# Low parts of the mixer's mx, mo and mv weights on GpSimd, and a later due count for a finished selection

## The chip, the cores and the metric

The kernel runs on one core of one Trainium2 chip. The metric is the device time of one execution in microseconds (us); a row of the trace gives times from the start of the profiled execution's span.

## The reference

A block of two layers (a causal convolution branch, a dilated attention branch, each with a gated per-layer embedding), then a feed-forward part (SwiGLU), a mixer, and a second feed-forward part, for 512 tokens of width 1024 in float32. The change lies in the mixer. It projects the normalised input to all that its two halves need, and the sparse attention half selects keys per query:

```python
def block(args):                       # 128 queries, block bi
    logits = jnp.einsum('bqhd,bsd->bqhs', iq_blk, ik)
    score = jnp.einsum('bqhs,bqh->bqs', jax.nn.relu(logits), iw_blk) * idx_scale
    score = jnp.where(allowed[None], score, -jnp.inf)
    # the k_sel = 128 largest scores of each query are the keys that it may attend to;
    # softmax attention of 8 heads (2 key/value heads) over those keys
...
# mLSTM half: mx -> causal convolution of 4 taps -> SiLU -> q, k;  mo -> sigmoid output gate;
# mv -> values;  input and forget gates from 8 more columns
# out = two gates * (attention @ wo, mLSTM @ wo) + residual
```

## The kernel before, in words

Every float32 weight comes from memory in pieces of 128x1024 elements (512 KB, "raw", four buffers) and is split into a high part `whi` and a low part `wlo` (six buffers each). ScalarE writes `whi` (L117, a rounding copy), and another engine writes `wlo = raw - whi` (L119). A product of 512 columns is then three matmuls, high by high, low by high and high by low (L281, L282, L283). In what follows ACT is ScalarE, DVE is VectorE, POOL is GpSimd and PE is TensorE.

`Stream.split` chooses the engine of `wlo`: GpSimd where the piece's index is in `POOL_LO`, its key in `POOL_KEYS` or its full name in `POOL_MORE` (most pieces of the feed-forward parts), and DVE otherwise. The mixer's pieces come as aq (queries), mx (mLSTM input), mo (output gate), mv (values), then the two gates gb and ga and the output weights.

The main products of a unit run in a loop that ticks; at each tick side work is given out at fixed rates. `k.t` counts main products. The side work of the attention half: `score(tb)` makes the index scores of query block tb (products L1079/L1080, rectified copies on ACT L1871, weighted sums on DVE L1878 and L1880); `select(tb)` takes the 128 largest by 16 rounds of a maximum of 8 (L1888) and a replacement (L1889) on DVE, and L1891 turns the result into an additive mask; `attend()` goes through 4 blocks of 8 heads in stages: s1 (products L1079/L1080 into a bank of PSUM), s1b (DVE adds the mask and takes the maximum, L1914, which also frees the bank; L1918 negates it; ACT takes the exponential, L1919), s2 (transposes L1932, ACT copies them, L1935), s3 (products with the values, L1948). `attend()` doesn't give out s1 of a block before its selection is in `SEL`. READY is 8, and two other kinds of results (the queries "AQ" among them) already become due that many main products after they were given out.

The mLSTM half: `mx_evac` scales each mx product into an SBUF tile (DVE, L1994), starts a convolution on ACT (L1998), adds three taps on DVE (L2002, two operands from SBUF) and takes the SiLU (L2004, its own ACT table, loaded by an `ACT_TABLE_LOAD`). The queries' norm goes through a sum on DVE (L1094, L1096), a power on GpSimd (L276) and a scaling (L1098, L1100); then PE transposes (L1850) and ACT and DVE split the result (L1069, L1070).

There are eight banks of PSUM. The order of the instructions on every engine is set by a scheduler with a timeline model when the kernel is built, so a change of an engine or of a due count moves instructions on all engines. Line numbers from L1893 on are larger by one after the change (L1914 becomes L1915).

Of the kernel before, what the change touches and what calls it, by code (L numbers as in the profile page):

```python
# [24 lines left out]
WBUFS = 6  # L25
FILL = 3
UNITS = ('aq', 'mx', 'mo', 'mv')
POOL_KEYS = ()
ROPE_AT = 5
PP_HEAD = 7  # L30
PP_MID = 11
# [24 lines left out]
class Stream:  # L56
# [22 lines left out]
    def split(self):  # L79
# [10 lines left out]
        self.parts[i] = self.two()  # L90
        pool = i in POOL_LO or key[0] in POOL_KEYS or key in POOL_MORE
        self.halves(self.parts[i], slice(0, nk * width), raw[:, :nk * width], pool)
# [955 lines left out]
def bc(ap, n, p=128):  # L1048

    return ap[:, :, None].to_broadcast([p, ap.shape[1], n])  # L1050
# [24 lines left out]
def mm2(k, ps, a, h, cols, b, keys):  # L1075


    t = a[h % 2][:, cols]
    k.nc.tensor.matmul(ps, t, b[0][:, keys], start=True, stop=False)  # L1079
    k.nc.tensor.matmul(ps, t, b[1 + h % 2][:, keys], start=False, stop=True)  # L1080
# [672 lines left out]
def mixer(k, nm, nm2):  # L1753
# [19 lines left out]
    allow0 = k.cp.tile([128, 128], F32, name="allow0")  # L1773
# [29 lines left out]
    AQ, MV, GS = {}, {}, {}  # L1803
    have = set()
# [52 lines left out]
    YA = []  # L1857

    def dsa():
        SEL = {0: allow0}  # L1860

        def score(tb):
            w = 128 * (tb + 1)
            sc = mem.get(width=w)
            RL = {}
            for h in range(9):
                if h < 8:
                    ps = ps_.get()
                    mm2(k, ps[:, :w], IQ[h // 2], h, slice(tb * 128, (tb + 1) * 128), IK, slice(0, w))
                    RL[h] = mem.get(width=w)  # L1870
                    nc.scalar.activation(RL[h], ps[:, :w], AF.Relu)  # L1871
                    ps_.put(ps)
                    yield w * 0.9e-3
                if h:
                    rl = RL.pop(h - 1)
                    iw = IW[:, tb, h - 1:h]
                    if h == 1:
                        V.tensor_scalar(sc, rl, iw, None, op0=OP.mult)  # L1878
                    else:
                        V.scalar_tensor_tensor(sc, rl, iw, sc, OP.mult, OP.add)  # L1880
                    mem.put(rl)
            V.memset(sc[0:64, w - 64:w], NEVER)
            return sc

        def select(tb, sc):
            for _ in range(TOPK // 8):
                m8 = k.small("m8", 8, 2)
                V.max(m8, sc)  # L1888
                V.match_replace(sc, m8, sc, GONE)  # L1889
                yield 0.3 + 2 * sc.shape[1] * 1e-3  # L1890
            V.tensor_scalar(sc, sc, GONE, NEG, op0=OP.not_equal, op1=OP.mult)  # L1891
            SEL[tb] = sc

        def attend():
            items = [(tb, h) for tb in range(4) for h in range(8)]
            st, blk = {}, {}

            def s1(it):
                tb, h = it
                w = 128 * (tb + 1)  # L1900
                if h == 0:
                    blk[tb] = {"md": k.small("amd", 16, 2)}
                ps = ps_.get()
                wide = max(w, 256)
                mm2(k, ps[:, :wide], AQ[tb], h, slice(h // 2 * 128, h // 2 * 128 + 128), AK[h // 4], slice(0, wide))
                st[it] = ps
                return w * 0.9e-3

            def s1b(it):
                tb, h = it  # L1910
                w = 128 * (tb + 1)
                md, ps = blk[tb]["md"], st[it]
                e = mem.get(width=w)
                V.tensor_tensor_reduce(out=e, in0=ps[:, :w], in1=SEL[tb], scale=1.0, scalar=-3.0e38, op0=OP.add,  # L1914
                                       op1=OP.max, accum_out=md[:, h:h + 1])  # L1915
                ps_.put(ps)
                ng = k.small("ang_", 1, 3)
                V.tensor_scalar(ng, md[:, h:h + 1], -0.125, None, op0=OP.mult)  # L1918
                nc.scalar.activation(e, e, AF.Exp, scale=0.125, bias=ng, accum_out=md[:, 8 + h:9 + h])  # L1919
                st[it] = e  # L1920
                if h == 7 and tb:
                    mem.put(SEL.pop(tb))
                if h == 7:
                    mem.put(*AQ.pop(tb))

            def s2(it):
                tb, h = it
                e = st[it]
                pt = ps_.get()
                w = 128 * (tb + 1)  # L1930
                for kb in range(tb + 1):
                    nc.tensor.transpose(pt[:, kb * 128:(kb + 1) * 128], e[:, kb * 128:(kb + 1) * 128], k.ident)  # L1932
                mem.put(e)
                t = mem.get(width=w)
                nc.scalar.activation(t, pt[:, :w], AF.Copy)  # L1935
                ps_.put(pt)
                st[it] = t
                return 0.11 * (tb + 1)

            def s3(it):  # L1940
                tb, h = it
                t = st.pop(it)
                B = blk[tb]
                if h == 0:
                    B["ps"] = ps_.get()
                g = h // 4
                for kb in range(tb + 1):
                    nc.tensor.matmul(B["ps"][:, h * 64:(h + 1) * 64], t[:, kb * 128:(kb + 1) * 128],  # L1948
                                     AV[kb][:, g * 64:(g + 1) * 64], start=(kb == 0), stop=(kb == tb))
                mem.put(t)  # L1950
                if h == 7:
                    rd = k.small("ard", 8, 2)
                    V.reciprocal(rd, B["md"][:, 8:16])
                    o = mem.get()
                    V.tensor_tensor(o.rearrange("p (h d) -> p h d", d=64),
                                    B["ps"].rearrange("p (h d) -> p h d", d=64), bc(rd, 64), OP.mult)
                    ps_.put(B["ps"])
                    YA.append(o)
                return 0.22 * (tb + 1)

            n = len(items)
            for i in range(n + DLAG[-1]):
                if i < n:
                    while items[i][0] not in AQ or items[i][0] not in SEL or ("s", 1) not in have:
                        yield 0.2
                    yield s1(items[i])
                if 0 <= i - DLAG[0] < n:
                    s1b(items[i - DLAG[0]])
                if 0 <= i - DLAG[1] < n:
                    yield s2(items[i - DLAG[1]])  # L1970
                if 0 <= i - DLAG[2] < n:
                    it = items[i - DLAG[2]]
                    yield s3(it)

        def scores():
            for tb in range(1, 4):
                while ("s", tb) not in have:
                    yield 0.2
                sc = yield from score(tb)
                yield from select(tb, sc)  # L1980
            mem.put(*[t for q in IQ for t in q], *IK)

        k.score_side = k.add_side(scores(), SCORE_RATE)
        yield from attend()
        mem.put(av, *AK[0], *AK[1])

# [186 lines left out]

    b_unit(k, "small", X, small_evac, 336)
    sd = k.add_side(dsa(), DSA_RATE)
    for u in UNITS:
        if u == UNITS[-1]:
# [77 lines left out]
READY = 8  # L2255
# [69 lines left out]
```

## Time and profile before

| what | value |
|---|---|
| three timed runs | 1782.2, 1781.98, 1779.75 us (median 1781.98) |
| the profiled execution | 1778.11 us, span 1776.0 us, mean TensorE clock 0.997 |
| busy share of the span | PE 99%, PEld 84%, DVE 71%, ACT 50%, POOL 36% |
| matmuls | 9480 on PE |

The span is the profiled execution from its first to its last recorded instruction; about 2 us of its time lie around it. The busy shares are averages over stages that differ.

### The profile page before, as it was taken

Reading aid. Unit: us, or ns where it says so; the run is one execution under the profiler, and the core shown is the slowest. Engines: PE = TensorE matmul, PEld = TensorE weight load, DVE = VectorE, ACT = ScalarE, POOL = GpSimd, SP = SyncE. Lnnn points to the kernel's source line nnn. Section 1 sums busy time; section 2 is a strip of 40 time slices with the busy share of each in tenths; the row PEclk is TensorE's granted clock in tenths of the full one; section 3 lists DMA queues with packets and bytes.
Section 4 is the critical chain, followed back from the end, with each engine's and each line's share of the span. In section 5 each row is a group of like instructions: output and inputs, shape, how many; then the busy total and the mean of one; then the engine's idle time right before and its main releaser. Section 6 shows DMA issues by size and latency. Waiting matters only on the chain. (4 is left out here: it accounts for less than half of the span.)

```text
span 1776.0 us, 25312 instructions
## 1 busy us (share of the span) xinstructions
PE 1749.3 (99%) x9480; PEld 1485.7 (84%) x9480; DVE 1259.0 (71%) x2372; ACT 893.4 (50%) x1561; POOL 642.2 (36%) x417
## 2 busy tenths in 40 slices
PE   8999999999999999999999999899999999999999
PEld 6876788888888888889999888678888888899897
DVE  6999667656466667977777659997447568777762
ACT  6776635565636543434443436577633335344342
POOL 5999220402030004466575401000000135656662
PEclk9999999999999999999999999999999999999999
DMA  7322233212322232143242632013242321333432
GB/s 203 108 74 83 60 95 116 75 54 67 119 60 84 72 94 73 44 127 115 85 131 66 183 109 90 24 48 96 60 130 85 93 83 54 114 99 94 128 90 65
DMA packets 262758, 162.14 MB, mean 91 GB/s; under 512 B 10256, under 2 KB 245100, under 8 KB 262636
## 3 DMA queue, kind: packets, MB, share of 16 engines
q1 hardware_dynamic: 262636, 160.53, 31.0%
q8 instruction: 74, 1.21, 0.3%
q14 instruction: 48, 0.39, 0.1%
HBM read 155.23 MB, written 5.28 MB: 90 GB/s over the span
## 5 line engine op out<-in xcount | busy, mean ns | idle before, releaser
L281 PE MATMUL b<-s,whi 128*128 128x512 f32 (+1 forms) x2240 | 786.4, 353 | 4.6 <-ACT s L640 3.4
L282 PE MATMUL b<-s,whi 128*128 128x512 f32 (+1 forms) x2240 | 788.6, 352 | 0.2 <-DVE s L296 0.2
L283 PE MATMUL b<-s,wlo 128*128 128x512 f32 (+1 forms) x2240 | 786.3, 351 | 0.0
L119 POOL TENSOR_TENSOR wlo<-raw,whi 128x512 fp32r<-128x512 f32 (+2 forms) x165 | 337.3, 2061 | 413.7 <-ACT whi L117 335.8
L281 PEld LDWEIGHTS b<-s,whi 128*128 128x128 f32 x2240 | 422.2, 189 | 64.8 <-ACT s L640 3.8
L282 PEld LDWEIGHTS b<-s,whi 128*128 128x128 f32 x2240 | 422.1, 188 | 62.2 <-issue 2.2
L283 PEld LDWEIGHTS b<-s,wlo 128*128 128x128 f32 x2240 | 422.5, 189 | 60.6 <-issue 1.2
L117 ACT ACTIVATE whi<-raw 128x1024 fp32r<-128x1024 f32 (+3 forms) x306 | 285.9, 945 | 358.1 <-PE b L282 206.8
L119 DVE TENSOR_TENSOR wlo<-raw,whi 128x1024 fp32r<-128x1024 f32 (+1 forms) x141 | 179.9, 1279 | 37.5 <-ACT whi L117 31.6
L281 PE MATMUL b<-whi,s 128*128 128x512 f32 (+1 forms) x416 | 172.2, 415 | 0.0
L282 PE MATMUL b<-wlo,s 128*128 128x512 f32 (+1 forms) x416 | 168.4, 405 | 0.0
L283 PE MATMUL b<-whi,s 128*128 128x512 f32 (+1 forms) x416 | 163.9, 394 | 0.0
L117 ACT ACTIVATE whi<-s 128x512 fp32r<-128x512 f32 x128 | 77.2, 627 | 154.8 <-DVE s L144 76.4
L735 POOL TENSOR_TENSOR s<-s,s 128x512 f32<-128x512 f32 x85 | 124.7, 1501 | 3.7 <-ACT s L731 2.6
L119 POOL TENSOR_TENSOR wlo<-s,whi 128x512 fp32r<-128x512 f32 x64 | 98.5, 1560 | 21.7 <-ACT whi L117 16.5
L1649 DVE TENSOR_TENSOR s<-b,s 128x256 f32<-128x256 f32 x192 | 76.1, 418 | 41.6 <-PE b L283 20.7
L737 DVE SCALAR_TENSOR_TENSOR b<-s,s,b 128x512 f32<-128x512 f32 x142 | 99.5, 747 | 4.0 <-ACT b L721 2.9
L276 POOL TENSOR_TENSOR h8y<-hv,mhalf 128x8 f32<-128x8 f32 x28 | 47.4, 1694 | 129.9 <-DVE hv L1096 112.4
L296 DVE TENSOR_TENSOR s<-s,s 128x512 fp32r<-128x512 f32 x84 | 88.5, 1075 | 4.7 <-ACT s L295 4.4
L283 PEld LDWEIGHTS b<-whi,s 128*128 128x128 f32 x416 | 78.7, 189 | 13.8
L281 PEld LDWEIGHTS b<-whi,s 128*128 128x128 f32 x416 | 78.9, 190 | 12.2 <-issue 0.2
L282 PEld LDWEIGHTS b<-wlo,s 128*128 128x128 f32 x416 | 79.1, 190 | 10.8 <-issue 0.2
(438 smaller groups left out, 2078.3 us busy)
## 6 DMA issues: line engine op xcount, KB each, us to landing
raw<-in_ffn_w_gate SPq DMA_DIRECT2D x44, 512.0 KB
raw<-in_ffn_w_up SPq DMA_DIRECT2D x44, 512.0 KB
raw<-in_attn_w_in SPq DMA_DIRECT2D x40, 512.0 KB
raw<-in_ffn_w_down SPq DMA_DIRECT2D x48, 384.0 KB
raw<-in_w_in SPq DMA_DIRECT2D x36, 512.0 KB
raw<-in_conv_w_in SPq DMA_DIRECT2D x24, 512.0 KB
raw<-in_ple_w_gate SPq DMA_DIRECT2D x16, 512.0 KB
raw<-in_conv_w_out SPq DMA_DIRECT2D x8, 512.0 KB
```

The costliest lines, as they stand in the source:

```text
L117: self.last_hi = self.k.nc.scalar.activation(hi, src, AF.Copy)
L119: eng.tensor_tensor(lo, src, hi.bitcast(F32), OP.subtract)
L276: self.nc.gpsimd.tensor_tensor(y, v, self.mhalf[:, :shape], OP.pow)
L281: mm(ps, a[0], b[0], start=first, stop=False)
L282: mm(ps, a[0], b[1], start=False, stop=False)
L283: self.last = mm(ps, a[1], b[0], start=False, stop=last)
L296: nc.vector.tensor_tensor(lo, src, hi.bitcast(F32), OP.subtract)
L735: nc.gpsimd.tensor_tensor(acc2, acc2, p, OP.add)
L737: nc.vector.scalar_tensor_tensor(acc, y[:, t:t + S], wcol(t, c), acc, OP.mult, OP.add)
L1649: add = lambda out, p, q, op=OP.add: V.tensor_tensor(out, p, q, op)
```

## The change

`POOL_KEYS` gets the three keys of the mLSTM half, so the 12 `wlo` of mx, mo and mv (128x1024 each) are written by GpSimd and not by DVE. And a selection counts as there only READY = 8 main products after its last instruction was given out.

```diff
-POOL_KEYS = ()
+POOL_KEYS = ('mx', 'mo', 'mv')
...
-        SEL = {0: allow0}
+        SEL, sel_due = {0: allow0}, {0: 0}
...
             SEL[tb] = sc
+            sel_due[tb] = k.t + READY
...
-                    while items[i][0] not in AQ or items[i][0] not in SEL or ("s", 1) not in have:
+                    while items[i][0] not in AQ or sel_due.get(items[i][0], k.t + 1) > k.t or ("s", 1) not in have:
```

The engine is chosen here, which is unchanged:

```python
        pool = i in POOL_LO or key[0] in POOL_KEYS or key in POOL_MORE
        self.halves(self.parts[i], slice(0, nk * width), raw[:, :nk * width], pool)
```

No other instruction is added but ACT table loads: the new order has 42 in all where there were 34. The order of the instructions moves as follows.

GpSimd, in the mixer, before (h3y and h8y are the queries' powers, nr and ny other powers; the memsets fill mLSTM tiles):

```order
L276 TENSOR_TENSOR nr<-nv,mhalf 128x4
L276 TENSOR_TENSOR h3y<-hv,mhalf 128x3 x4
L276 TENSOR_TENSOR h8y<-hv,mhalf 128x8 x4
L2017 MEMSET s_11622 64x512
L2017 MEMSET s_11286 64x512
```

The same place after the change:

```order
L276 TENSOR_TENSOR nr<-nv,mhalf 128x4
L276 TENSOR_TENSOR h3y<-hv,mhalf 128x3 x3
L119 TENSOR_TENSOR wlo<-raw,whi 128x1024 x2
L276 TENSOR_TENSOR h3y<-hv,mhalf 128x3
L276 TENSOR_TENSOR h8y<-hv,mhalf 128x8 x3
L119 TENSOR_TENSOR wlo<-raw,whi 128x1024 x4
L276 TENSOR_TENSOR h8y<-hv,mhalf 128x8
L119 TENSOR_TENSOR wlo<-raw,whi 128x1024 x4
L2018 MEMSET s_11602 64x512
L119 TENSOR_TENSOR wlo<-raw,whi 128x1024 x2
L2018 MEMSET s_11266 64x512
```

The 12 `wlo` stand between the powers, and the last power of the queries now stands behind four of them in a row.

DVE before, where the first taps of the convolution stand (s_10478 is the mx tile that they add into, s_10091 the scores of block 1, hv the sum that the last power takes):

```order
L119 TENSOR_TENSOR wlo<-raw,whi 128x1024
L1888 MAX m_10209<-s_10091 128x8
L119 TENSOR_TENSOR wlo<-raw,whi 128x1024
L1994 TENSOR_TENSOR s_10475<-b_10289,s_9759 128x512
L1094 TENSOR_REDUCE hv<-s_10347 128x8
L1889 MATCH_REPLACE s_10091<-m_10209,s_10091 128x256
L119 TENSOR_TENSOR wlo<-raw,whi 128x1024
L1096 TENSOR_SCALAR hv<-hv,r2m 128x8
L2002 SCALAR_TENSOR_TENSOR s_10478<-s_10475,pc,s_10478 128x512
L1888 MAX m_10216<-s_10091 128x8
```

The same place after the change:

```order
L1995 TENSOR_TENSOR s_10475<-b_10289,s_9759 128x512
L1094 TENSOR_REDUCE hv<-s_10347 128x8
L1888 MAX m_10277<-s_10091 128x8
L1096 TENSOR_SCALAR hv<-hv,r2m 128x8
L2003 SCALAR_TENSOR_TENSOR s_10478<-s_10475,pc,s_10478 128x512
L1889 MATCH_REPLACE s_10091<-m_10277,s_10091 128x256
L2003 SCALAR_TENSOR_TENSOR s_10478<-s_10475,pc,s_10478 128x512
L1888 MAX m_10286<-s_10091 128x8
```

The low parts are gone from DVE, and the taps and the rounds of the selection stand closer.

ACT before, at the rectified copies of block 2's scores (the tile s_10478 again; b_10431 is a bank of PSUM with one head's scores):

```order
L1998 ACTIVATE s_10478<-s_10475,pc 128x512
L1871 ACTIVATE s_10394<-b_10391 128x384
L1871 ACTIVATE s_10409<-b_10406 128x384
L117 ACTIVATE whi<-raw 128x1024
L1871 ACTIVATE s_10434<-b_10431 128x384
L1871 ACTIVATE s_10440<-b_10437 128x384
L1069 ACTIVATE s_10450<-b_10445,pc 64x512
```

The same place after the change:

```order
L1999 ACTIVATE s_10478<-s_10475,pc 128x512
L117 ACTIVATE whi<-raw 128x1024
L1871 ACTIVATE s_10394<-b_10391 128x384
L1871 ACTIVATE s_10409<-b_10406 128x384
L2005 ACT_TABLE_LOAD
L2005 ACTIVATE s_10478<-s_10478 128x512
L117 ACTIVATE whi<-raw 128x1024
L1920 ACT_TABLE_LOAD
L1920 ACTIVATE s_10414,amd<-s_10414,ang__10416 128x128
L1920 ACTIVATE s_10422,amd<-s_10422,ang__10424 128x128
L1069 ACTIVATE s_10450<-b_10445,pc 64x512
L1871 ACTIVATE s_10434<-b_10431 128x384
```

The SiLU of the first mx tile, a `whi`, two table loads and two exponentials moved ahead of the copy that empties b_10431.

PE before, where the attention of block 1 begins (b_10852 and b_10761 are banks of mo products, b_10706 and its neighbours take scores of block 1):

```order
L281 MATMUL b_10852<-whi,s_9617 128x512
L282 MATMUL b_10852<-wlo,s_9617 128x512
L283 MATMUL b_10852<-whi,s_9618 128x512
L1079 MATMUL b_10792<-s_9810,s_10453 128x256
L1080 MATMUL b_10792<-s_9812,s_10453 128x256
L1079 MATMUL b_10706<-s_9805,s_10453 128x256
L1080 MATMUL b_10706<-s_9807,s_10453 128x256
L1079 MATMUL b_10733<-s_9810,s_10450 128x256
L1080 MATMUL b_10733<-s_9811,s_10450 128x256
L281 MATMUL b_10761<-whi,s_9434 128x512
```

The same place after the change (b_10655 is the last bank of mx, b_10852 the first of mo):

```order
L283 MATMUL b_10655<-s_9617,wlo 128x512
L1933 MATMUL b_10692<-ident,s_10616 128x128
L1079 MATMUL b_10675<-s_9805,s_10450 128x256
L1080 MATMUL b_10675<-s_9806,s_10450 128x256
L1079 MATMUL b_10706<-s_9805,s_10453 128x256
L1080 MATMUL b_10706<-s_9807,s_10453 128x256
L1079 MATMUL b_10733<-s_9810,s_10450 128x256
L1080 MATMUL b_10733<-s_9811,s_10450 128x256
L1949 MATMUL b_10510<-s_9820,s_10666 128x64
L1933 MATMUL b_10717<-ident,s_10659 128x128 x2
L281 MATMUL b_10852<-whi,s_9434 128x512
```

The scores of block 1 moved from behind the first mo product to ahead of it.

## Rows read from the trace of the kernel before

**Rows 1.** The page's head and its busy times by engine.

```profile
span 1776.0 us, 25312 instructions
...
PE 1749.3 (99%) x9480; PEld 1485.7 (84%) x9480; DVE 1259.0 (71%) x2372; ACT 893.4 (50%) x1561; POOL 642.2 (36%) x417
```

**Rows 2.** Stretches: busy us (count) of PE, PEld, DVE, ACT, POOL; granted clock; DMA; GB/s.

```profile
1080.00:1100.00 20.00, 20.00 (x95) 16.36 (x95) 19.62 (x49) 10.66 (x15) 3.71 (x2) 1.00 0.38 117
1094.00:1140.00 46.00, 37.47 (x176) 30.62 (x175) 44.55 (x134) 29.61 (x65) 2.07 (x1) 0.93 0.26 79
1140.00:1330.00 190.00, 189.84 (x992) 156.77 (x991) 127.85 (x292) 118.19 (x219) 6.13 (x8) 1.00 0.27 78
1220.00:1240.00 20.00, 20.00 (x114) 16.88 (x113) 10.61 (x22) 17.41 (x35) 0.00 (x0) 1.00 0.30 80
```

**Rows 3.** Timeline of PE: start, time, line, tiles, [idle before, releaser].

```profile
1100.63 0.60 PE L1850 MATMUL b<-ident,s 128*128 128x128 f32 x4
...
1135.71 0.38 PE L1079 MATMUL b<-s,s 128*128 128x256 f32 x1 [4.50 <-DVE amd L1914]
...
1136.65 0.63 PE L281 MATMUL b<-whi,s 128*128 128x512 f32 x1
1137.07 0.63 PE L282 MATMUL b<-wlo,s 128*128 128x512 f32 x1
...
1139.58 0.39 PE L282 MATMUL b<-wlo,s 128*128 128x512 f32 x1
1139.81 0.40 PE L283 MATMUL b<-whi,s 128*128 128x512 f32 x1
```

**Rows 4.** Timeline of DVE.

```profile
1075.54 0.49 DVE L1880 SCALAR_TENSOR_TENSOR s<-s,iw,s 128x256 f32<-128x256 f32 x1
...
1134.57 0.28 DVE L1891 TENSOR_SCALAR s<-s 128x256 f32<-128x256 f32 x1
```

**Rows 5.** Timeline of ACT.

```profile
1087.16 3.03 ACT L117 ACTIVATE whi<-raw 128x1024 fp32r<-128x1024 f32 x3
...
1099.62 0.91 ACT L1871 ACTIVATE s<-b 128x384 f32<-128x384 f32 x2
1100.48 0.69 ACT L1069 ACTIVATE s<-b,pc 64x512 fp32r<-64x512 f32 x1
1101.44 0.40 ACT L1919 ACTIVATE s<-s,ang__10416 128x128 f32<-128x128 f32 x1 [0.27 <-DVE ang__10416 L1918]
...
1103.83 1.28 ACT L2004 ACT_TABLE_LOAD   x1
1105.12 0.64 ACT L2004 ACTIVATE s<-s 128x512 f32<-128x512 f32 x1
```

**Rows 6.** Timeline of GpSimd in the attention layer.

```profile
693.15 10.08 POOL L119 TENSOR_TENSOR wlo<-raw,whi 128x1024 fp32r<-128x1024 f32 x4 [5.65 <-ACT whi L117]
```

**Rows 7.** Timeline of DVE in the same stretch.

```profile
695.16 8.74 DVE L1612 SCALAR_TENSOR_TENSOR s<-s,pc,s 128x256 f32<-128x256 f32 x5
...
704.43 2.45 DVE L1612 SCALAR_TENSOR_TENSOR s<-s,pc,s 128x256 f32<-128x256 f32 x6
```

**Rows 8.** Groups on DVE, 1040 to 1320: busy, mean ns, idle before.

```profile
L119 DVE TENSOR_TENSOR wlo<-raw,whi 128x1024 fp32r<-128x1024 f32 x37 | 45.0, 1219 | 3.0 <-ACT whi L117 2.8
...
L2002 DVE SCALAR_TENSOR_TENSOR s<-s,pc,s 128x512 f32<-128x512 f32 x12 | 8.9, 743 | 0.0
...
L1888 DVE MAX8 m<-s 128x8 f32<-128x256 f32 x16 | 6.8, 423 | 0.2
...
L1880 DVE SCALAR_TENSOR_TENSOR s<-s,iw,s 128x384 f32<-128x384 f32 x7 | 4.3, 609 | 0.0
...
L1994 DVE TENSOR_TENSOR s<-b,s 128x512 f32<-128x512 f32 x4 | 2.8, 691 | 0.9 <-PE b L283 0.8
```

**Rows 9.** Timeline of GpSimd in the mixer.

```profile
1074.40 1.89 POOL L276 TENSOR_TENSOR h8y<-hv,mhalf 128x8 f32<-128x8 f32 x1 [2.66 <-DVE gze L2067]
...
1097.89 2.07 POOL L276 TENSOR_TENSOR h8y<-hv,mhalf 128x8 f32<-128x8 f32 x1 [12.03 <-DVE hv L1096]
```

## The prediction

> **What bounds the kernel now.** The page says first which engine is full: PE is busy for 99% of the span, DVE for 71%, GpSimd for 36% [rows 1]. So the change can help only where PE waits or runs at its lower clock. The windows show where that is in the mixer: from 1094 to 1140 us PE is busy for 37.47 of 46.00 us at a mean granted clock of 0.93, and from 1140 to 1330 it is busy for 189.84 of 190.00 at 1.00 [rows 2]. The gain to be had is thus in the first stretch; behind it there is only something to lose. The idle time there is 46.00 − 37.47 = 8.5, and the clock costs 0.07 × 46 = 3.2. Counted from start to start of the matmuls, against the undisturbed step of each shape, the stretch loses 14.1 us; the other 2.4 are tails of matmuls that nothing overlaps at a stop, and short waits. I count in this way below.
>
> PE's timeline names the largest loss: a product L1079 waits 4.50 us, until 1135.71, for a bank that DVE's mask and maximum (L1914) must empty [rows 3]. DVE's timeline says why that is late: the mask of block 1 is ready (L1891) at 1134.57 [rows 4]. After this stop PE runs at the lower of its levels (1.2 and 2.4 GHz): a matmul starts 0.42 us after the one before, later 0.23 [rows 3]. DVE itself is busy for 19.62 of 20.00 us from 1080 on, and for 44.55 of 46.00 from 1094 on [rows 2]. It is the queue that delays the selection.
>
> **The change part by part.** *The low parts.* One `wlo` takes 1.22 us on DVE [rows 8], some 1.14 from start to start. By the order, ten of the twelve stood before the end of the first selection: ten times 1.14 is 11.4 us off that queue. Thirteen more DVE instructions move behind the end (four taps at 0.74, an L1994 at 0.69, one round's maximum at 0.42 [rows 8], and others of this kind): 6.3 us. The selection would end 17.7 us earlier, at 1134.8 − 17.7 = 1117.1, if nothing new delayed DVE. The 4.50 us and the slow matmuls behind them are gone even if half of this is lost again.
>
> On GpSimd four `wlo` in a row took 10.08 us, 2.52 each [rows 6]. Twelve are 30 us on an engine that works for only 2.07 of the 46 us and 6.13 of the next 190 [rows 2]. They are prepared a few products ahead, and PE is at 20.00 of 20.00 from 1080 on [rows 2]. I cost their later end at nothing, with split buffers as the cover; the two last, mv2 and mv3, have by my reckoning 2 to 5 us in hand.
>
> *What GpSimd does to DVE.* At 693.15 four `wlo` run on GpSimd [rows 6], and beside them five L1612 of DVE, with two tensors from SBUF, took 8.74 us, where the next six took 2.45 [rows 7]. That is one L1612 for each `wlo`, not 0.41 us each. Such an instruction waits for the `wlo` that runs. Before, no `wlo` ran on GpSimd where the mixer's taps (L2002) and sums (L1880) run, so no row shows it there. The bounds: below, no wait at all; above, one whole `wlo`, 2.5 us, per tap, sum or `hv` scaling issued while one runs. I take nearly the upper end, since the instruction of [rows 7] has the same form as the taps (two SBUF tensors and a column).
>
> The Trainium skill states this as a rule (page "SBUF — State Buffer", section "SBUF: two separate sides"): DVE and GpSimd share a pair of ports that one instruction locks for its whole length, for a DVE instruction with two SBUF inputs against a GpSimd one that reads SBUF. The rows on `wlo` agree. Another row does not: GpSimd's power at 1074.40 takes 1.89 us [rows 9], it reads SBUF, and the L1880 that starts inside it takes 0.49 [rows 4]. By the rule a tap would wait for the power behind the four `wlo` too, about 1 us, and the sum would be +3 instead of +2; by the row it doesn't, and I go by the row.
>
> *The first stop.* Three high parts end by 1087.16 + 3.03 = 1090.2 [rows 5], the first near 1088.2; the fourth follows at once. Four `wlo` then fill GpSimd from 1088.2 to 1098.3 (10.1, as in [rows 6]). The first tap of tile s_10478 waits for that end and takes 0.74 [rows 8]; the second follows a replacement, at 1099.9. Behind them GpSimd runs the power of the last queries, 2.07 [rows 9], to 1100.5, and the `wlo` of mo2 to 1103.0. The third tap, behind four instructions, falls into that one and ends at 1103.8. The order puts ACT's SiLU of this tile, and all behind it, before the copy that empties bank b_10431. From 1103.8: SiLU 0.64 [rows 5], a `whi` 1.0, a table load 1.28, two exponentials of 0.4 with their sums (0.6 each), L1069 0.69, half of the pair L1871 at 0.91, 0.46 [rows 5]: 5.3 us with some gaps less overlap, 1108.6 to 1109.1; I take 1108.6. PE reaches the transposes L1850 of b_10456 near 1100.8 (before, such transposes stand at 1100.63 [rows 3]), and they need the same bank. They wait until 1108.7: 7.9 us. The clock behind it costs what it did behind the 4.50: eight matmuls at 0.42 instead of 0.23, 1.5 us.
>
> *The second stop.* PE then has the 24 matmuls of mx's last product but one and some score products. DVE gets that bank, and ahead of the next exponential of block 0 stand a scaling L1995 0.69, two sums at 0.61, a maximum 0.42, a tap 0.74 [rows 8], two maskings of some 0.3 and small ones: 3.7. Then the exponential itself, 0.4 [rows 5], less what PE has left to do in between. I take 3.9 from start to start, 1.0 for the clock behind it, 0.5 for a short wait ahead of it.
>
> *The selection now.* 1117.1, and DVE's waits (taps, `hv`, sums) of 9.7: 1126.9. The scores of block 1, moved ahead of mo's first product, meet an exponential that four more table loads of 1.28 [rows 5] have delayed: 0.7 us of wait.
>
> *The due count.* READY = 8 main products are 8 × 3 × 0.23 = 5.6 us at most by which the attention of a block is given out later. It moves blocks 2 and 3 some 20 PE rows back; both sides end well ahead of the output weights, so I cost it at nothing. If that cover were gone, it would be those 5.6.
>
> *Behind 1140.* The eight more table loads cost ACT 8 × 1.28 = 10.3 us; ACT is busy for 17.41 of 20.00 us from 1220 on [rows 2]. Between nothing and three loads on the path (3.8) I take half a load, 0.6, since ACT still has 2.6 us free there.
>
> **The sum.** After: 7.9 + 1.5 + 0.5 + 3.9 + 1.0 + 0.7 = 15.5; before: 14.1. That is +1.4, and with 0.6 behind it +2.0. The profiled execution took 1778.11 us, so 1780.1 in its terms; the median of the runs is 3.9 above it (1781.98), which gives 1784.0.
>
> **The rivals.** *R1, DVE isn't held up by GpSimd in the mixer* (faster). For it: instructions of DVE that read a bank of PSUM or one tensor, the rounds of the selection too, are no such instructions, and most of the queue is of that kind. Against it: [rows 7]. It decides at a tap of less than 2 us beside a running `wlo`. The copy that empties b_10431 then ends 5.7 earlier, at 1102.9 (a load, a SiLU and two exponentials are still ahead of it); the first stop is 2.3, the others shrink little, and the stretch loses 8.5 to 10.5 instead of 14.1: 3.6 to 5.6 less. With 4.6: 1777.4.
>
> *R2, ACT becomes the bound behind 1140* (slower). All of the forecast's stops, and of the 17 loads from 1210 to 1300 (14 before) the three new ones fall between a product's bank and PE: 3 × 1.28 and 1.4 of clock, +5.3: 1789. For it: ACT's 17.41 of 20.00 there [rows 2]; against: PE had not a single idle time there. It decides where ACT's busy share reaches 20 of 20. A late `wlo` of mv2 or mv3 would cost 1 to 2 and the clock, and give nearly the same time.
>
> *R3, nothing changes*: the stops trade places and the sum is near zero. That is the middle of the forecast's own range, 1780 to 1787, and has no chance of its own.
>
> **How the numbers follow.** A measurement of this kernel can tell about 0.2%, 3.6 us: faster is below 1778.4, slower above 1785.5. The forecast has a chance of 0.45 (same 0.31, slower 0.12, faster 0.02, since the two stops, 7.9 and 3.9, are each known to some 2 us). R1 has 0.30 (faster 0.23, same 0.07): the row that speaks against it is clear, but my order of events at the first stop has many links. R2 has 0.25 (slower 0.23, same 0.02). Together: faster 0.25, same 0.40, slower 0.35. The range takes R1's larger gain with a little more (5.6 below 1782 is 1776.4, so 1775) and R2's 1789.
>
> **What would show it.** Right: taps L2003 and a scaling L1096 of DVE that take over 2 us beside GpSimd's `wlo` between 1088 and 1104; an idle time of PE of 6 to 9 us ahead of an L1850 near 1109, released by ACT's L1871; the 4.50 before L1079 gone, with L1891 of block 1 at 1123 to 1130; GpSimd's `wlo` at 2.4 to 2.8 us; no idle time of PE from 1150 to 1330. Wrong: taps of 0.75 and no large stop near 1105 (R1); idle times of PE released by ACT from 1210 to 1300 (R2). What would upset all of it is an order on ACT or PE that runs otherwise than I followed it, above all a copy of b_10431 that isn't what L1850 waits for.

## The result and the profile after

The changed kernel takes 1788.72 us (median of 6 runs, 1786.68 to 1789.81), the kernel before, run beside it, 1779.26 (6 runs): a ratio of 1.0053, 95% interval 1.0042 to 1.0063. It is slower by 9.5 us. The profiled execution took 1788.9 us with a span of 1786.8, 10.8 longer than that of before [rows 1]; 1.6 of this lies in the first 100 us, where nothing is changed.

The windows of the kernel after (columns as in [rows 2]) show two places of loss:

```profile
1094.00:1140.00 46.00, 36.21 (x153) 29.07 (x152) 42.29 (x114) 30.75 (x60) 17.46 (x8) 0.78 0.28 81
1140.00:1330.00 190.00, 186.37 (x970) 153.91 (x969) 129.93 (x297) 125.06 (x229) 13.73 (x11) 0.99 0.23 64
1160.00:1180.00 20.00, 16.49 (x77) 13.04 (x76) 19.16 (x40) 11.67 (x20) 5.72 (x3) 0.97 0.23 57
1200.00:1330.00 130.00, 130.00 (x690) 109.07 (x689) 75.61 (x173) 87.23 (x159) 4.55 (x5) 1.00 0.26 74
```

From 1094 to 1140 PE is idle for 9.8 us, little more than the 8.5 before, but the clock is down to 0.78 from 0.93 [rows 2]. It is down in two places:

```profile
1104.67:1117.15 12.48, 9.37 (x27) 7.28 (x28) 12.31 (x34) 8.68 (x20) 4.31 (x2) 0.50 0.33 100
1117.15:1127.39 10.24, 7.69 (x44) 6.42 (x42) 9.36 (x22) 5.21 (x12) 2.48 (x1) 1.00 0.04 6
1127.39:1134.32 6.93, 6.92 (x18) 5.35 (x19) 6.80 (x26) 6.65 (x13) 0.00 (x0) 0.51 0.23 69
```

A second loss, 3.5 us of idle time, lies between 1160 and 1180, where PE had no idle time before. From 1200 on PE is never idle. Counted from start to start of the matmuls, the loss is 20.2 us against 14.9 from 1094 to 1144, 0.8 against 1.9 to 1160, 8.5 against 3.6 to 1200, and 12.8 against 12.7 to 1340: +5.3 − 1.1 + 4.9 + 0.1 = 9.2, about the 9.5 of the runs. These counts are estimates: they depend on the step that is taken as undisturbed.

PE's timeline after, at the stops:

```profile
1104.67 1.11 PE L1850 MATMUL b<-ident,s 128*128 128x128 f32 x4 [3.95 <-DVE amd L1915]
...
1108.48 0.69 PE L1079 MATMUL b<-s,s 128*128 128x384 f32 x1 [1.42 <-DVE amd L1915]
...
1111.97 1.11 PE L1850 MATMUL b<-ident,s 128*128 128x128 f32 x4 [1.57 <-ACT s L1871]
...
1113.74 0.63 PE L281 MATMUL b<-s,whi 128*128 128x512 f32 x1
1114.16 0.63 PE L282 MATMUL b<-s,whi 128*128 128x512 f32 x1
...
1117.15 0.41 PE L283 MATMUL b<-s,wlo 128*128 128x512 f32 x1
1117.40 0.39 PE L281 MATMUL b<-s,whi 128*128 128x512 f32 x1
...
1127.39 0.86 PE L1933 MATMUL b<-ident,s 128*128 128x128 f32 x2 [1.81 <-ACT s L1920]
...
1177.25 0.66 PE L1949 MATMUL b<-s,s 128*128 128x64 f32 x4 [3.51 <-ACT s L1936]
```

The 4.50 us of [rows 3] are gone. In their place PE stops three times from 1100.7 to 1112, with small products in between, and once more, for 1.81 us, until 1127.39. Its steps of 512 columns are 0.42 to 0.43 us (the 1.2 GHz level) until 1117.15; after that they are 0.22 to 0.25.

DVE's timeline after says what was late:

```profile
1098.50 1.35 DVE L1096 TENSOR_SCALAR hv<-hv,r2m 128x8 f32<-128x8 f32 x1
1099.77 2.92 DVE L2003 SCALAR_TENSOR_TENSOR s<-s,pc,s 128x512 f32<-128x512 f32 x1
...
1103.01 0.73 DVE L2003 SCALAR_TENSOR_TENSOR s<-s,pc,s 128x512 f32<-128x512 f32 x1
...
1104.75 2.42 DVE L2003 SCALAR_TENSOR_TENSOR s<-s,pc,s 128x512 f32<-128x512 f32 x1
...
1109.94 1.30 DVE L1098 TENSOR_SCALAR h8y<-h8y,nr 128x8 f32<-128x8 f32 x1
...
1124.12 2.10 DVE L2003 SCALAR_TENSOR_TENSOR s<-s,pc,s 128x512 f32<-128x512 f32 x1
...
1130.41 0.29 DVE L1891 TENSOR_SCALAR s<-s 128x256 f32<-128x256 f32 x1
...
1168.44 2.38 DVE L1880 SCALAR_TENSOR_TENSOR s<-s,iw,s 128x512 f32<-128x512 f32 x1
...
1171.09 2.20 DVE L1891 TENSOR_SCALAR s<-s 128x384 f32<-128x384 f32 x1
...
1173.87 0.14 DVE L1919 TENSOR_SCALAR ang__11024<-amd 128x1 f32<-128x1 f32 x1
```

And GpSimd's:

```profile
1092.64 9.50 POOL L119 TENSOR_TENSOR wlo<-raw,whi 128x1024 fp32r<-128x1024 f32 x4 [3.97 <-ACT whi L117]
1102.05 2.40 POOL L276 TENSOR_TENSOR h8y<-hv,mhalf 128x8 f32<-128x8 f32 x1
1104.15 2.47 POOL L119 TENSOR_TENSOR wlo<-raw,whi 128x1024 fp32r<-128x1024 f32 x1
1108.86 2.35 POOL L119 TENSOR_TENSOR wlo<-raw,whi 128x1024 fp32r<-128x1024 f32 x1 [2.24 <-ACT whi L117]
1123.19 2.48 POOL L119 TENSOR_TENSOR wlo<-raw,whi 128x1024 fp32r<-128x1024 f32 x1 [11.98 <-ACT whi L117]
...
1167.86 5.21 POOL L119 TENSOR_TENSOR wlo<-raw,whi 128x1024 fp32r<-128x1024 f32 x2 [5.73 <-ACT whi L117]
```

And ACT's:

```profile
1107.20 0.63 ACT L2005 ACTIVATE s<-s 128x512 f32<-128x512 f32 x1 [5.37 <-DVE s L2003]
...
1111.45 0.84 ACT L1871 ACTIVATE s<-b 128x384 f32<-128x384 f32 x2
...
1174.09 1.28 ACT L1920 ACT_TABLE_LOAD   x1 [4.88 <-DVE ang__11024 L1919]
```

The long taps and the mask of DVE end 0.2 to 0.6 us, no more than their own length, after a low part on GpSimd does: the first tap at 1102.69, after the run of four (1102.14); the third at 1107.17, after mo2's (1106.62); the mask L1891 at 1173.29, after mv3's (1173.07). The tap at 1103.01, beside the power, takes its 0.73. The queue behind them does the rest: at 1104.67 PE waits for maskings L1915 that stand behind the taps, and ACT's SiLU (with a `whi`, a table load and two exponentials behind it) waits for the third tap. The stop of 1.81 has the same origin: the tap at 1124.12 lasts through mv0's low part, and the exponential that PE waits for comes behind it. PE itself waits for no low part in the mixer.

### The profile page after: what moved, and what is told of

Same layout as the page of the kernel before. It is cut to its first block, busy times and chain, and to the rows that moved or that the text cites. A ratio compares the mean times of both kernels' runs of the same rounds, so it can differ in the third digit from the quotient of the medians.

```text
span 1786.8 us, 25349 instructions
## 1 busy us (share of the span) xinstructions
PE 1756.0 (98%) x9480; PEld 1491.2 (83%) x9480; DVE 1261.9 (71%) x2360; ACT 902.6 (51%) x1569; POOL 671.1 (38%) x429
## 4 chain that ended last, share of the span: by engine, by line
PE 86%; DVE 5%; POOL 4%; ACT 2%; issue 2%; DMA 1%; SPq 0%; ACTq 0%; POOLq 0%; DVEq 0%
PE b L282 26%; PE b L281 26%; PE b L283 26%; POOL s L735 4%; PE b L1306 1%; PE b L1363 1%; PE b L1343 1%; PE b L1949 1%; DVE s L2003 1%; ACT whi L117 1%; PE b L1250 1%; DVE s L1889 1%; DVE s L1880 1%; DVE m L1888 1%; DMA raw<-in_conv_w_in 1%
## 5 line engine op out<-in xcount | busy, mean ns | idle before, releaser
L119 POOL TENSOR_TENSOR wlo<-raw,whi 128x1024 fp32r<-128x1024 f32 (+2 forms) x177 | 367.2, 2093 | 454.3 <-ACT whi L117 378.1
L119 DVE TENSOR_TENSOR wlo<-raw,whi 128x1024 fp32r<-128x1024 f32 (+1 forms) x129 | 167.1, 1298 | 37.3 <-ACT whi L117 31.6
L1649 DVE TENSOR_TENSOR s<-b,s 128x256 f32<-128x256 f32 x192 | 75.9, 417 | 41.2 <-PE b L283 20.2
```

The lines of the kernel that those rows point to most:

```text
L119: eng.tensor_tensor(lo, src, hi.bitcast(F32), OP.subtract)
L1649: add = lambda out, p, q, op=OP.add: V.tensor_tensor(out, p, q, op)
```

## Experiments

Two theories were put against each other. Theory L: a low part on GpSimd holds up those instructions of DVE that take two tensors from SBUF (taps, weighted sums) or scale a tensor from SBUF to SBUF. Theory O: the new order of the instructions (table loads ahead of copies, a later due count) costs by itself. All ratios are to the kernel before, run on the same chip.

**The two halves of the change.** The due count alone:

```diff
-POOL_KEYS = ('mx', 'mo', 'mv')
+POOL_KEYS = ()
```

> Only the due count of the selection; all twelve low parts stay on DVE. Theory L: the late due count costs nothing or little, since DVE isn't held up: 1776 to 1783, with the 4.5 us stop near 1135 still there or moved. Rival O (the later due count and the order that follows from it make the loss): 1785 or more.

It took 1778.30, ratio 0.9994 (0.9985 to 1.0003): no change; the stop is still there, 4.15 us at 1138.71. The engine alone, an edit of the kernel before:

```diff
-POOL_KEYS = ()
+POOL_KEYS = ('mx', 'mo', 'mv')
```

> Only the engine of the twelve low parts; a selection counts at once, as before. Theory L: nearly all of the loss is here: 1785 to 1791, taps of over 2 us beside GpSimd's low parts, stops near 1104 and 1173. Rival O: near the kernel before, 1776 to 1782.

It took 1790.81, ratio 1.0063 (1.0050 to 1.0075), with taps of 2.93 and 2.43 us and a stop of 3.92 at 1105.38. The second stop did not come near 1173, as expected, but at 1186.12 (2.12 us): there the last pair on GpSimd, 1175.63 to 1180.37, holds up a low part of DVE, which takes 3.38 instead of 1.22. The whole loss comes with the engine. The due count changes nothing that these intervals can tell.

**The order kept, the cause taken away.**

```diff
-            eng.tensor_tensor(lo, src, hi.bitcast(F32), OP.subtract)
+            eng.memset(lo.bitcast(F32), 0.0) if pool == "mix" else eng.tensor_tensor(lo, src, hi.bitcast(F32), OP.subtract)
```

> The changed kernel, but GpSimd sets the twelve low parts of mx, mo and mv to zero instead of computing them, so it reads no SBUF for them; the low-part term of these weights is left out of the result. The order of the instructions at the first stop stays that of the changed kernel (a SiLU, a high part, two table loads ahead of the copy that frees the bank). Theory L: taps back to 0.75 us, the idle time near 1104 falls from 6.9 us to under 3, the 3.5 us at 1173 go, and the run takes 1773 to 1780. Rival O (the new order is what costs): stops stay, 1785 to 1790.

It took 1774.13, ratio 0.9974 (0.9963 to 0.9985). Its groups on DVE from 1040 to 1320 (busy, mean ns):

```profile
L2003 DVE SCALAR_TENSOR_TENSOR s<-s,pc,s 128x512 f32<-128x512 f32 x12 | 8.9, 741 | 0.1
```

And the same group in the kernel after:

```profile
L2003 DVE SCALAR_TENSOR_TENSOR s<-s,pc,s 128x512 f32<-128x512 f32 x12 | 15.5, 1291 | 0.6 <-ACT s L1999 0.6
```

With nearly the same order of ACT at the first stop, and the third tap of DVE a little earlier in its order, the taps take 0.74 us, and PE's idle time near 1104 is 1.02 and 0.70. One stop of 3.35 remains at 1119, and the 3.51 near 1177 are gone. Theory O fails as the cause of the loss. The memset is shorter too (0.95 against 2.47) and waits for no `whi`: one memset ends at 1094.13 and the next starts at 1100.18, so none runs beside the first three taps (1095.57 to 1098.69). This run thus takes the neighbour away altogether, and GpSimd's own lateness with it; by itself it does not tell holding up from lateness. The next one does.

**The cost by itself.** A first kernel set seven instructions of DVE beside four settings of GpSimd. One of the settings, the tap beside low parts:

```python
    for _ in range(4): G.tensor_tensor(lo, raw, hi.bitcast(F32), OP.subtract)
    for _ in range(8): V.scalar_tensor_tensor(c, x[:, 1:513], col, c, OP.mult, OP.add)
```

> This kernel computes nothing of the block and stores zeros; it only sets each of seven instructions of DVE beside a run of GpSimd instructions: nothing, four low parts (128x1024 subtraction), four memsets of that size, or eight powers of 128x8. Theory L (GpSimd holds DVE up): the tap (two tensors from SBUF, 128x512) takes about 0.74 us alone and about 2.5 for the first ones beside a low part, as does the scaling of 8 columns (0.2 alone, over 1 beside it); the product from PSUM (0.69), the maximum of 8 (0.42) and the replacement (0.41) stay as they are; beside memset and power the tap stays at 0.74. Rival P (by the page's rule on the shared ports): the tap waits for the power as well, 1.6 us each. Rival O (the stops came from the order, not from GpSimd): all of them within 20% of their time alone in every setting.

Its instructions came out mixed over the settings, so that powers and low parts alternate on GpSimd; it shows the wait (taps of 2.7 to 4.1 us beside low parts) but can't tell settings apart. The second has a barrier between the settings:

> Computes nothing of the block; zeros are stored. The settings of the earlier measurement, now one after the other with a barrier of all engines between them, so that each DVE instruction has only one kind of GpSimd instruction beside it (L37 to L49 alone, L52 to L70 beside low parts, L73 to L91 beside memsets, L94 to L112 beside powers). Theory L: beside low parts the tap and the two scalings from SBUF wait (about 2.4 us for each low part, so 8 taps take 8 to 10 us more), product from PSUM, maximum, replacement and sum don't; beside powers nothing waits. Rival P: beside powers the tap waits 1.6 us for each power as well. The memset: by the same wait, the taps stay and the 512-wide scaling waits.

Its groups on DVE (busy, mean ns): lines 37, 39, 41 alone, 52 to 70 beside low parts, 73 to 79 beside memsets, 94 and 97 beside powers.

```profile
L52 DVE SCALAR_TENSOR_TENSOR c<-x,col,c 128x512 f32<-128x512 f32 x8 | 13.8, 1731 | 0.3
L58 DVE TENSOR_SCALAR w<-x 128x512 f32<-128x512 f32 x8 | 11.5, 1436 | 0.3
L55 DVE TENSOR_SCALAR m<-m 128x8 f32<-128x8 f32 x12 | 10.2, 851 | 0.4
L79 DVE TENSOR_SCALAR w<-x 128x512 f32<-128x512 f32 x8 | 6.2, 780 | 0.3
L94 DVE SCALAR_TENSOR_TENSOR c<-x,col,c 128x512 f32<-128x512 f32 x8 | 6.0, 752 | 0.3
L73 DVE SCALAR_TENSOR_TENSOR c<-x,col,c 128x512 f32<-128x512 f32 x8 | 6.0, 752 | 5.8 <-SPq L35 5.6
L37 DVE SCALAR_TENSOR_TENSOR c<-x,col,c 128x512 f32<-128x512 f32 x8 | 6.0, 752 | 5.6 <-SPq L35 5.3
...
L61 DVE TENSOR_TENSOR w<-ps,x 128x512 f32<-128x512 f32 x8 | 5.5, 691 | 0.4
...
L67 DVE MAX8 m<-sc 128x8 f32<-128x256 f32 x8 | 3.4, 428 | 4.3 <-SPq L35 4.1
...
L41 DVE TENSOR_SCALAR w<-x 128x512 f32<-128x512 f32 x8 | 3.4, 427 | 0.3
...
L70 DVE MATCH_REPLACE8 sc<-m,sc 128x256 f32<-128x256 f32 x8 | 3.3, 409 | 0.0
...
L97 DVE TENSOR_SCALAR m<-m 128x8 f32<-128x8 f32 x12 | 2.1, 173 | 8.9 <-SPq L35 8.6
L39 DVE TENSOR_SCALAR m<-m 128x8 f32<-128x8 f32 x12 | 2.1, 171 | 0.5
```

And on GpSimd the powers beside taps (L93) and beside products from PSUM (L102):

```profile
L93 POOL TENSOR_TENSOR hy<-hv,hw 128x8 f32<-128x8 f32 x8 | 14.1, 1762 | 0.9 <-SPq L35 0.3
...
L102 POOL TENSOR_TENSOR hy<-hv,hw 128x8 f32<-128x8 f32 x8 | 13.1, 1635 | 0.7 <-SPq L35 0.2
```

Beside low parts the tap goes from 0.752 to 1.731, and the scalings from SBUF from 0.427 to 1.436 and from 0.171 to 0.851 on the mean of 8 or 12 (four low parts are spread over them). The product from PSUM, the maximum and the replacement are as alone. Beside powers and beside memsets the tap keeps 0.752; the scaling waits beside a memset too (0.780). This is theory L, shown where nothing waits for anything but the engines themselves; rival P falls for powers by themselves. It is the power that is longer beside taps, by 0.13 us on the mean (1.762 against 1.635).

**Which low parts.** The changed kernel with one key alone, and with the last pair back on DVE. The first of the four edits (the next two have 'mo' and 'mv' alone; the last has 'mx' and 'mo', and ('mv', 0) and ('mv', 1) in POOL_MORE):

```diff
-POOL_KEYS = ('mx', 'mo', 'mv')
+POOL_KEYS = ('mx',)
```

> The changed kernel, but only the four low parts of mx on GpSimd. Theory L: they run before the taps begin and end by 1093 to 1095, so few DVE instructions of the kind that waits stand beside them; DVE has 4.6 us less ahead of the first selection, the stop near 1135 shrinks from 4.5 us or goes: 1774 to 1779. Rival O: moved order alone, 1779 to 1785.

> The changed kernel, but only the four low parts of mo on GpSimd. Theory L: these run beside the taps and sums of 1093 to 1110, which take over 2 us there, the first stop stays at 3 us or more, that at 1173 is gone: 1778 to 1786. Rival O: near the kernel before.

> The changed kernel, but only the four low parts of mv on GpSimd. Theory L: the pair mv2 and mv3 runs beside the sums of block 3 and holds up the mask of block 2, as in the changed kernel: a stop of 2 to 4 us of PE near 1160 to 1175, the stop of 4.5 near 1135 still there or shorter: 1780 to 1786. Rival O: within 2 us of the kernel before.

> The changed kernel with the last two low parts (mv2, mv3) back on DVE; ten stay on GpSimd. Theory L with two separate stops: the stop of 3.5 us near 1173 goes with its slow matmuls, the first stops stay: 3.5 to 5 us less than the changed kernel, 1783.5 to 1786. If the second stop were a consequence of the first ones or of the order: 1787 to 1790.

| on GpSimd | us | ratio (interval) |
|---|---|---|
| mx | 1779.52 | 1.0000 (0.9991 to 1.0008) |
| mo | 1777.09 | 0.9982 (0.9973 to 0.9991) |
| mv | 1783.09 | 1.0022 (1.0013 to 1.0030) |
| all but mv2, mv3 | 1787.15 | 1.0042 (1.0029 to 1.0054) |

mv alone has the second loss without the first: 7.6 us from start to start between 1160 and 1200 where before has 3.6, with a stop of 1.83 at 1175. mx missed its expectation by half a microsecond, and lies where the moved order alone was expected. Its two later low parts (1093.89 to 1099.66 on GpSimd) hold up one of mo's on DVE, which takes 3.08 us instead of 1.22, and the stop near 1135 is 2.57 us at 1139.00. In this run PE is idle for 9.4 us from 1094 to 1140, nearly as long as in the changed kernel, and the clock stays up:

```profile
1094.00:1140.00 46.00, 36.63 (x181) 29.11 (x180) 45.16 (x121) 30.08 (x58) 7.29 (x3) 1.00 0.31 92
```

mo was better than expected: its run of three ends at 1098.88 and holds up the scaling L1096 (1.31), and the taps behind it take 0.74. The three alone add up to 1.5 us (0.1 − 2.3 + 3.7), all together cost 9.5: it is together that mx and mo make the run of four that lasts into the taps.

With mv2 and mv3 back on DVE the stop at 1177 is 0.61 instead of 3.51, and the loss between 1160 and 1200 goes from 8.5 to 4.6. So in the trace it comes from this pair, as theory L has it. But the time fell by 1.6, not by 3.5 to 5, and lies in the range that was set for the rival case, a stop that follows from the first ones or from the order. PE's timeline of this run shows a new stop:

```profile
1234.07 0.43 PE L1949 MATMUL b<-s,s 128*128 128x64 f32 x2 [2.12 <-ACT s L1936]
```

ACT works there almost without a break from 1221.20 to 1234.96, with three table loads of 1.28. That is rival R2, in a variant of the change and not in the change itself.

**A version to keep?** mo alone without the due count (the key in the kernel before), and mo with the two early pieces of mx:

```diff
-POOL_KEYS = ('mx', 'mo', 'mv')
+POOL_KEYS = ('mo',)
...
-POOL_MORE |= {("fd", l, p, m) for l in (1, 2) for p in range(len(FFN_PARTS)) for m in range(8)}
+POOL_MORE |= {("fd", l, p, m) for l in (1, 2) for p in range(len(FFN_PARTS)) for m in range(8)} | {('mx', 0), ('mx', 1)}
```

> The kernel before with only the four low parts of mo on GpSimd, and no due count of the selection. Theory L: the gain of the version with both (1777.1) comes from the four low parts that DVE no longer has ahead of the first selection: 1775 to 1779. If the due count is needed for it: 1779 or more.

> The due count, with the low parts of mo and of mx0 and mx1 on GpSimd. The two of mx run near 1062, ahead of the taps, where DVE is not full. Theory L: at most the gain of mo alone and up to 2 us more: 1774 to 1778. If what counts is how the stretch from 1094 to 1140 happens to be ordered: anything from 1774 to 1785.

They took 1778.21 (0.9994, 0.9985 to 1.0002) and 1780.02 (1.0005, 0.9996 to 1.0014). The first has the same stops from 1094 to 1140 as mo with the due count, within 0.2 us each; the two intervals overlap, so whether the due count adds anything is open. The second missed (1774 to 1778), in the range for a gain that hangs on the order: there the first tap is issued at 1099.46, 2 us before mo's run of three ends (1101.43), and takes 2.52; PE stops for 4.08 us until 1103.96. With mo alone it is issued at 1098.83, as that run ends (1098.88). Here two us of order decide between a gain and none. mo with the due count is the best of the kernels that compute everything, 2.3 us ahead of the kernel before.

## Why the prediction was right and where it was off

The time lies in the range, just below its upper end of 1789, and "slower" had a chance of 0.35. The likeliest case was "same", at 1784.0 and 1780 to 1787; the kernel is 4.7 us above that. That the time lies in the range is in part luck: the forecast stood on 1781.98, the median of three runs of the kernel before, and six runs give 1779.26. As a difference +2.0 was forecast and +9.5 measured, more than the +7 of R2, the slowest case. The mechanism was the forecast's; three terms of its sum were mis-sized.

- *What GpSimd does to DVE* held. A tap was to wait up to one low part; the taps took 2.92 and 2.42. The row of before that decided, another instruction of the same form some 400 us earlier, was enough. R1, which denied it, set −4.6 for its own case; the memset run, which takes the low parts and their lateness away, gained 5.3.
- *The first stop*: 7.9 was forecast as one wait for the copy L1871. It came as three, 3.95 + 1.42 + 1.57 = 6.94, the first two for DVE's maskings. The size was near, the releaser right only for the last. The size is in part luck: the run of four began at 1092.64, not at 1088.2, so everything behind it was some 3 to 4 us later than followed (the copy freed PE at 1111.97, not at 1108.7), and products that PE could do in between filled that time. *The second stop*: 3.9 and 0.5 were forecast, 0.54 + 0.20 + 1.81 = 2.55 came, the 1.81 behind a tap of 2.10 that the forecast had at 0.74.
- *The clock behind the two stops* gave the first two terms that failed: 1.5 and 1.0 us were set down, the first by what one stop of 4.50 had cost. PE was at its lower level from 1104.67 to 1117.15 (granted clock 0.50) and from 1127.39 to 1134.32 (0.51). Less the two waits inside, the first is 9.5 us of work at half the clock, up to 4.7 us lost; the second costs some 3. By this estimate the two are 5 us above the forecast, and the shorter waits, counted from start to start, take some 1.5 of it back: about the difference between the +1.4 forecast for this stretch and the +5.3.
- *The low parts of mv2 and mv3* are the third. Their later end was costed at nothing, and R2 gave them 1 to 2 us for being late. They were not late. They held up DVE a second time: the sum L1880 and the mask L1891, and with them the negated maximum, a table load and the exponential that PE waits for, where no idle time of PE was to come from 1150 to 1330. +4.9. The forecast had the rule and followed it only as far as the low part of mo2.
- *The selection* came at 1130.41, not at 1126.9 (the sum is 1126.8), 0.4 us behind the range given (1123 to 1130). The wait of 4.50 is gone, as said. *The due count* costs nothing, as said.
- *Behind 1140*: 0.6 was set down for the table loads; +0.1 was measured from 1200 on. R2 did not happen in this kernel.
- The Trainium skill (page "SBUF — State Buffer", section "SBUF: two separate sides") has the rule that decided, and the isolated rows agree for low parts, for PSUM operands and for the memset, which holds up the scaling but not the tap. For the power they differ, as the row of before did: the tap keeps 0.752 beside powers that read SBUF. The measurement decides, and the extra 1 us by the rule did not come.

## What to carry to other kernels

Before moving elementwise work from DVE to GpSimd, list what DVE does at that time. Here taps, weighted sums, low parts and scalings from SBUF waited until the low part that ran on GpSimd ended; products from PSUM, the selection's maximum and replacement didn't. Follow every moved instruction to its place, the last pair too. And price the work that PE does at its lower level, not the stops alone: the stops of 3.95, 1.42 and 1.57 us left 12.5 us at that level, the one of 4.50 before some 3.5, and the stops of mx alone, 9.4 us in all and none above 2.57, left none. Neither the number of the stops nor their sum gives that price here.

## What was not expected of the hardware

A scaling of only 8 columns waits as well: L1096 took 1.35 us and L1098 1.30 beside low parts, against 0.22 each in the run with memsets, where GpSimd is idle beside them. And where powers and low parts alternate on GpSimd, a tap issued inside a power waited through the rest of it and the whole low part behind it. In the first kernel of the isolated cost, DVE's row:

```profile
95.65 4.08 DVE L63 SCALAR_TENSOR_TENSOR c<-x,col,c 128x512 f32<-128x512 f32 x1
```

GpSimd's recorded power lasts there from 94.80 to 96.88 and the low part behind it to 99.19. Why it waited there, and neither beside powers alone nor at 1103.01 in the mixer (0.73, a power with a low part behind it), stays open.
